# Second half's output projection as seven block products, with sums and scalings made on POOL

## The chip, the cores and the metric

The kernel runs on one core of one Trainium2 chip. TensorE (PE), VectorE (DVE), ScalarE (ACT), GpSimd (POOL) and the DMA issuer SyncE (SP) each work through a queue of their own in order, and wait for one another by semaphores. The metric is the device time of one launch, in microseconds (us), the median of several runs.

## The reference, cut to what matters

One layer with two token mixers over x of 2048 tokens by 2048 features, all in float32:

```python
h = rms_norm(x, norm_w)
q, k, v, z_attn, u, z_ssm = split(h @ w_in)       # 1024, 256, 256, 1024, 1024, 1024 columns
o_attn = swa_sink_attention(q, k, v, ...) * silu(z_attn)
y = gelu(s5_ssm(u, ...));  y = y * sigmoid(y @ w_glu + b_glu)
o_ssm = y * silu(z_ssm)
merged = concat(rms_norm(o_attn, w_a), rms_norm(o_ssm, w_s))   # 1024 + 1024 features
x = x + merged @ w_out                                          # w_out 2048 x 2048
```

Attention looks back over a window of 128 tokens. The state space part runs a linear recurrence over all tokens, done here in 32 pairs of channel groups.

## The kernel before

The tokens are worked in two halves of 1024 (`HT`). Every float32 product is made of three matmuls: each operand is split into a rounded high part and a low rest (`xh`, `xl` for activations, `wh`, `wl` for weights), and high x high, high x low and low x high are added in PSUM. A weight block comes by one DMA on SP's queue into `wr` (ring of three), ACT rounds it into `wh`, DVE subtracts into `wl` (`w_unit`, L308).

A panel is a stretch of such matmuls with one PSUM accumulation: `panel_feat` (L319) has 24 matmuls of 512 columns for each weight block, `panel_tok` (L335) 48 of 256 columns. A panel's four PSUM banks (`psg`) are free again when its results have been read out by its `evac`. Order of the program in `run` (L1021):

- half 0: panels for u, q/k/v and z_attn. Beside them `setup_all` (L1086) prepares the rope tables, the norm of half 1 and the tables of the state space part (`ssm_setup`, L588; its rotation tables start from two small POOL memsets, `Ct` and `St`, L757). Then the z_ssm panels of half 0 and the u panels of half 1, with attention of half 0 beside them (`attend_all`, L499). `x_later` (L295) loads half 1's transposed x in between, scales it by weight and row factor on DVE and splits it.
- half 1: z_attn, q/k/v and z_ssm panels, with `ssm_pairs` (L779) beside them: for each of 32 pairs a load, a split, PE, a scan on DVE, PE again, and a gelu. Its memory pool takes the place of half 0's attention pool.
- the half-GLU of half 0 (`glu`, L911) with `tail_attn` (L880) beside it, the output panels of half 0 (`out_panel`) with attention of half 1 beside them, the half-GLU of half 1 with its `tail_attn`, and at last `out_wide` (L965) for half 1: 4 column blocks x 2 groups of features x 8 weight blocks x 24 matmuls = 1,536 matmuls of 512 columns.

Attention needs POOL: a memset of the first key tile `kst` (L478), the sums `vt` and `dv` (L517 to L520) and the masked product `pm` (L566) are POOL instructions. In the kernel before POOL issues no DMA at all.

"Beside" is set by `weave` (L990): after so many steps of the panels it takes one step of the side work, at a raised priority. A scheduler then fixes, before the program runs, the order of the instructions on each engine's queue; on the chip no engine departs from it.

## Time and profile before

| | us |
|---|---|
| median of three runs (2880.41 to 2883.33) | 2881.29 |
| the profiled execution, its own time | 2882.15 |
| its span on the core | 2880.4 |
| PE busy in the span | 2800.6 |
| DVE, ACT, POOL busy | 1774.8, 1046.9, 154.9 |

The profiled execution lies 0.03% above the median, and 1.75 us of its time lie outside the span. Matmul ends are modelled, so a busy PE is not PE at its peak: the pace is read from the count of matmuls in a stretch. Idle time of an engine that is not the bottleneck costs nothing by itself.

### The profile page before, as it was taken

How to read it: one execution, taken by the hardware profiler on the slowest of the kernel's cores; microseconds unless marked ns; L12 is line 12 of the kernel's file. 1: busy time of each engine (PE TensorE's matmuls, PEld its weight loads, DVE VectorE, ACT ScalarE, POOL GpSimd, SP SyncE). 2: the span in 40 equal slices, each digit the busy share in tenths (PEclk: the TensorE clock that was granted, in tenths of full speed). 3: DMA queues.
4: the chain of work that ended last, by engine and by line, in shares of the span. 5: the costliest groups of instructions: out<-in, count | busy, mean ns of one | idle time of the engine just before them, and what ended most of it. 6: DMA issues, size and time to landing. Idle time of an engine off the chain costs nothing.

```text
span 2880.4 us, 45277 instructions
## 1 busy us (share of the span) xinstructions
PE 2800.6 (97%) x16992; PEld 2502.1 (87%) x16992; DVE 1774.8 (62%) x4171; ACT 1046.9 (36%) x2377; POOL 154.9 (5%) x316
## 2 busy tenths in 40 slices
PE   6999999989999999999999999998999999999999
PEld 5879999878888788888999988878999999778887
DVE  6682746855553955677678984377777755842222
ACT  6411222134552554333333332355555533521110
POOL 0000000001110111000000000000112210000000
PEclk9999999999999999999999999999999999999999
DMA  5842536553332542645355555333444444333321
GB/s 176 241 116 67 158 92 169 144 141 110 98 107 80 184 117 86 164 138 153 119 153 154 160 146 152 107 121 98 148 136 126 125 138 155 99 103 106 106 80 56
DMA packets 421292, 369.36 MB, mean 128 GB/s; under 512 B 53200, under 2 KB 377296, under 8 KB 421072
## 3 DMA queue, kind: packets, MB, share of 16 engines
q1 hardware_dynamic: 419008, 366.45, 43.0%
q8 instruction: 134, 2.20, 0.3%
q14 instruction: 86, 0.70, 0.1%
q10 hardware_dynamic: 2064, 0.01, 0.0%
HBM read 271.03 MB, written 99.55 MB: 129 GB/s over the span
## 4 chain that ended last, share of the span: by engine, by line
PE 77%; DVE 10%; DMA 8%; issue 2%; SPq 2%; ACT 1%; POOL 0%; ACTq 0%; POOLq 0%; DVEq 0%
PE psg L329 30%; PE psg L347 27%; PE psg L974 6%; PE pss L974 3%; DMA oa<-OA 2%; PE pss L531 2%; PE pst L974 2%; PE pso L974 1%; DVE ml L93 1%; DVE yg L84 1%; PE pso L571 1%; PE pso L569 1%; PE pst L557 1%; DVE wl L84 1%; DMA TCS<-St 1%
## 5 line engine op out<-in xcount | busy, mean ns | idle before, releaser
L84 DVE TENSOR_TENSOR wl<-wr,wh 128x512 fp32r<-128x512 f32 x456 | 314.9, 691 | 593.6 <-ACT wh L315 574.5
L315 ACT CAST wh<-wr 128x512 fp32r<-128x512 f32 x456 | 282.1, 619 | 981.4 <-PE psg L329 301.4
L329 PE MATMUL psg<-xh,wl 128*128 128x512 f32 x1536 | 492.9, 394 | 4.8 <-DVE wl L84 4.7
L329 PE MATMUL psg<-xh,wh 128*128 128x512 f32 x1536 | 494.5, 395 | 2.2 <-ACT wh L315 1.3
L329 PE MATMUL psg<-xl,wh 128*128 128x512 f32 x1536 | 493.7, 395 | 2.1 <-DVE xl L84 2.1
L347 PE MATMUL psg<-wl,xh 128*128 128x256 f32 x1536 | 435.1, 284 | 0.9 <-DVE wl L84 0.9
L347 PE MATMUL psg<-wh,xh 128*128 128x256 f32 x1536 | 434.1, 284 | 0.0
L347 PE MATMUL psg<-wh,xl 128*128 128x256 f32 x1536 | 433.5, 284 | 0.0
L329 PEld LDWEIGHTS psg<-xh,wl 128*128 128x128 f32 x1536 | 287.5, 189 | 64.6 <-DVE wl L84 7.4
L329 PEld LDWEIGHTS psg<-xh,wh 128*128 128x128 f32 x1536 | 288.1, 190 | 60.1 <-ACT wh L315 1.8
L329 PEld LDWEIGHTS psg<-xl,wh 128*128 128x128 f32 x1536 | 287.6, 189 | 59.6 <-DVE xl L84 3.6
L347 PE MATMUL psg<-wh,mh 128*128 128x256 f32 x1024 | 289.1, 285 | 7.8 <-ACT tt L922 7.8
L347 PEld LDWEIGHTS psg<-wl,xh 128*128 128x128 f32 x1536 | 294.2, 192 | 1.3 <-DVE wl L84 1.3
L347 PEld LDWEIGHTS psg<-wh,xh 128*128 128x128 f32 x1536 | 293.8, 192 | 0.1
L347 PEld LDWEIGHTS psg<-wh,xl 128*128 128x128 f32 x1536 | 293.5, 192 | 0.0
L347 PE MATMUL psg<-wl,mh 128*128 128x256 f32 x1024 | 290.8, 285 | 0.6 <-DVE wl L84 0.6
L347 PE MATMUL psg<-wh,ml 128*128 128x256 f32 x1024 | 288.8, 285 | 0.0
L347 PEld LDWEIGHTS psg<-wh,mh 128*128 128x128 f32 x1024 | 195.2, 192 | 8.0 <-ACT tt L922 8.0
L347 PEld LDWEIGHTS psg<-wl,mh 128*128 128x128 f32 x1024 | 196.1, 192 | 0.8 <-DVE wl L84 0.8
L347 PEld LDWEIGHTS psg<-wh,ml 128*128 128x128 f32 x1024 | 195.2, 192 | 0.0
L548 ACT ACTIVATE sm<-pss,mx,rs 128x128 f32<-128x128 f32 x240 | 108.4, 458 | 50.3 <-DVE mx L84 49.9
L84 POOL TENSOR_TENSOR pm<-ph,sel 128x256 fp32r<-128x256 f32 x120 | 95.4, 795 | 516.1 <-ACT ph L560 498.6
(403 smaller groups left out, 4662.3 us busy)
## 6 DMA issues: line engine op xcount, KB each, us to landing
wr<-in_w_in_dram SPq DMA_DIRECT2D x296, 256.0 KB
wr<-in_w_out_dram SPq DMA_DIRECT2D x128, 256.0 KB
tb<-TCS SPq DMA_DIRECT2D x64, 256.0 KB
xr<-in_x_dram SPq DMA_DIRECT2D x64, 256.0 KB
out_dram<-xr SPq DMA_DIRECT2D x64, 256.0 KB
raw<-MBC SPq DMA_DIRECT2D x32, 384.0 KB
kst<-KK SPq DMA_DIRECT2D x56, 192.0 KB
xst<-in_x_dram SPq DMA_DIRECT2D x16, 512.0 KB
```

Of the source, the lines that this page charges most:

```text
L84: (eng or self.nc.vector).tensor_tensor(out=out, in0=a, in1=b, op=op)
L93: self.nc.vector.scalar_tensor_tensor(out=out, in0=a, scalar=s, in1=b, op0=op0, op1=op1)
L315: nc.scalar.copy(hi, raw)
L329: nc.tensor.matmul(ps[t], wt[:, kk, :], xx[k][:, t * 512:(t + 1) * 512], start=(k == 0 and i == 0), stop=(k == nkc - 1 and i == 2))
L347: nc.tensor.matmul(o, xx[k][:, sl], wt[:, kk, :], start=(k == 0 and i == 0 and t % 2 == 0), stop=(k == nkc - 1 and i == 2), skip_group_che ...
L531: nc.tensor.matmul(ps[:, h * 256:h * 256 + 256], qst[:, bq % 2, hp * 2 + h, :], kst[:, i, ksl], start=(h == 0 and i == 0), stop=(i == 1), ...
L548: nc.scalar.activation(sm[:, h, :], sc[:, h, :], AF.Exp, scale=rs[:, h:h + 1], bias=negm[:, h:h + 1], accum_out=den[:, h:h + 1])
L557: nc.tensor.transpose(pt[:, h * P:(h + 1) * P], sm[:, h, :], self.ident)
L569: nc.tensor.matmul(po, vst[:, blk, :], pp, start=(i == 0), stop=False)
L571: nc.tensor.matmul(po, dv[:, blk, :], pm[:, i], start=False, stop=(i == 1))
L974: nc.tensor.matmul(ps[t], xx[k0 + k][:, t * P:(t + 1) * P], wt[:, 0, :], start=(k == 0 and j == 0), stop=(k == 7 and j == 2))
```

## The change

The second half's output projection is a 1024 x 2048 by 2048 x 2048 product. Seen as 2 x 2 blocks (token half x feature group on one side, feature group x column half on the other) it had eight block products; now it has seven, each of 512 tokens x 1024 features x 1024 columns, between sums and differences of blocks, as in Strassen's scheme (Winograd's form). Four of the seven need sums of weight blocks (`T1` to `T4`); `out_sums` makes them early, in `setup_all`: 32 units of 256 columns, each with six loads, four stores and four additions, all on POOL and POOL's queue. The rows of the two feature groups have to be scaled before blocks can be mixed, so `attn_scale` multiplies half 1's attention by its row factor and writes it to DRAM (`OAN`), 16 times load, multiply, store, again on POOL; the state space part is scaled on DVE (`form_ssm`). The rest of the operands are formed on DVE and ACT as side work of the products. Half 1's x is scaled by its row factor on POOL as well (`x_scaled`, 16 loads, multiplies, stores to `XN`), and `x_later` only applies the weight. Half 1's attention adds up its squares in `attend` (on POOL) in place of `tail_attn`; that attention is spread over 0.7 of the panels in place of 0.5. In the half-GLU the product with silu(z) is written in natural token order, so that what follows runs on whole rows. In all 384 DMAs are put on POOL's queue: 320 for the weight sums (128 KB each), 32 for x, 32 for attention.

```diff
@@ x_scaled is new, x_later shorter
+    def x_scaled(self, pool, half):
         rb = pool.tile([P, HT], F32, tag="rb", name="rb")
         self.spread(self.rstd[:, half * 8:half * 8 + 8], rb, pool)
         for k in range(NK):
+            x = pool.tile([P, HT], F32, tag="xs", name="xs", bufs=2)
+            self.nc.gpsimd.dma_start(x, self.a["xT"][k * P:(k + 1) * P, half * HT:half * HT + HT])
+            self.tt(x, x, rb, ALU.mult, self.nc.gpsimd)
+            self.nc.gpsimd.dma_start(self.XN[k], x)
+            yield
+
+    def x_later(self):
...
-            self.stt(x, x, self.nw[:, k:k + 1], rb, ALU.mult, ALU.mult)
-            nc.scalar.copy(self.xh[k], x)
-            self.tt(self.xl[k], x, self.xh[k].bitcast(F32), ALU.subtract)
+            self.ld.dma_start(x, self.XN[k])
+            w = self.nw[:, k:k + 1]
+            nc.scalar.activation(self.xh[k], x, AF.Copy, scale=w)
+            self.stt(self.xl[k], x, w, self.xh[k].bitcast(F32), ALU.mult, ALU.subtract)
@@ ssm_setup, in the loop over the rotation tables
+                for _ in range(4):
+                    next(xs, None)
                 yield
@@ new: scaled attention, and its use
+    def attn_scale(self, pool):
+        for k in range(8):
+            for c in (0, 512):
+                o = pool.tile([P, 512], F32, tag="on", name="on")
+                self.nc.gpsimd.dma_start(o, self.OA[k * P:(k + 1) * P, HT + c:HT + c + 512])
+                self.tt(o, o, self.rba[:, c:c + 512], ALU.mult, self.nc.gpsimd)
+                self.nc.gpsimd.dma_start(self.OAN[k, :, c:c + 512], o)
+            yield
+    def form_a11(self):
+        for k in range(8):
+            self.split_to(0, k, self.attn_scaled(k, 0, 512), self.aow[:, k:k + 1])
+            yield
@@ new: weight sums (w_block(q) is a block of w_out for q < 4, else of WT)
+    def out_sums(self, pool):
+        nc = self.nc
+        g = nc.gpsimd
+        for u in range(32):
+            k, c = u // 4, u % 4 * 256
+            x, y = (pool.tile([P, 256], F32, tag=f"ws{i}", name=f"ws{i}") for i in range(2))
+            get = lambda t, q: g.dma_start(t, self.w_block(q, k, c, 256))
+            put = lambda i, t: g.dma_start(self.WT[i, k, :, c:c + 256], t)
+            get(x, 1)
+            get(y, 0)
+            self.tt(x, x, y, ALU.subtract, g)
+            put(0, x)
+            get(y, 3)
+            self.tt(y, y, x, ALU.subtract, g)
+            put(1, y)
+            yield
+            get(x, 2)
+            self.tt(x, y, x, ALU.subtract, g)
+            put(3, x)
+            get(x, 1)
+            get(y, 3)
+            self.tt(y, y, x, ALU.subtract, g)
+            put(2, y)
+            yield
@@ new: one block product
+    def product(self, slot, q, evac, *sides):
...
+            ps = [self.psg() if n == 0 else self.psa() for t in range(4)]
+            for k in range(8):
+                raw = self.wp.tile([P, 512], F32, tag="wr", name="wr")
+                self.ld.dma_start(raw, self.w_block(q, k, n * 512, 512))
...
+                for t in range(4):
+                    sl = slice(o + t * P, o + t * P + P)
+                    for j, (xx, wt) in enumerate(((self.sh[c], hi), (self.sh[c], lo), (self.sl[c], hi))):
+                        nc.tensor.matmul(ps[t], xx[:, sl], wt, start=(k == 0 and j == 0), stop=(k == 7 and j == 2))
...
+            for t in range(4):
+                evac(n, t, ps[t])
@@ new: strassen_out, its seven calls; out_wide is gone
+        self.product(0, B11, e1, (self.form_s3(), 8, 0), (ssm, 5, 6))
+        self.product(1, T3, e7, (ssm, 5, 0), (s2, 3, 10))
+        self.product(2, B21, e2, (s2, 5, 0))
+        self.product(0, T2, e6, (s1, 8, 0))
+        self.product(1, T1, e5, (s4, 8, 0))
+        self.product(2, B22, e3, (a22, 8, 0))
+        self.product(0, T4, e4)
@@ run
-            self.weave(o0[:-1], self.attend_all(pool, 1), 33, 0.0, 0.5, PA)
+            self.asq = pool.tile([P, HT], F32, tag="asq", name="asq")
+            self.weave(o0[:-1], self.attend_all(pool, 1), 33, 0.0, 0.7, PA)
+            self.ra = self.row_scale(pool, self.asq, 1.0, "ra")
...
-            self.weave(o0[-1:])
-            self.glu(1, pool, yin, self.tail_attn(1, pool, 0), 8)
...
+            self.spread(self.ra, self.rba, pool)
...
+            self.weave(o0[-1:], self.attn_scale(pool), 8, 0.0, 1.0, 0)
+            self.glu(1, pool, yin, self.form_a11(), 8)
+            self.strassen_out(pool)
@@ setup_all
-        yield from self.ssm_setup()
+        with self.tc.tile_pool(name="bg", bufs=1) as pool:
+            sums = self.out_sums(pool)
+            for _ in self.ssm_setup():
+                for _ in range(3):
+                    next(sums, None)
+                yield
```

In `strassen_out` a result is read out of PSUM by DVE, added to x on POOL and stored; the last product (`e4`) ends the kernel so.

How the order on the queues changes, at three places. First POOL, from the tables' last memsets to the first attention instructions (`ws` are the tiles of the weight sums, `WT` their place in DRAM). Before:

```order
L757 MEMSET Ct 128x8
L758 MEMSET St 128x8
L478 MEMSET kst 128x2x128
L84 TENSOR_TENSOR vt<-vst 128x128
L84 TENSOR_TENSOR vt<-vt 128x64
L84 TENSOR_TENSOR dv<-vt,dv 128x64
L84 TENSOR_TENSOR vt<-vst 128x192
L84 TENSOR_TENSOR vt<-vt 128x128
```

Now, the last rows ahead of the first attention instruction:

```order
L1007 DMA WT<-ws_6076 128x256
L1006 DMA ws_6075<-in_w_out_dram 128x256
L87 TENSOR_TENSOR ws_6075<-ws_6076,ws_6075 128x256
L1007 DMA WT<-ws_6075 128x256
L1006 DMA ws_6076<-in_w_out_dram 128x256
L1006 DMA ws_6075<-in_w_out_dram 128x256
L87 TENSOR_TENSOR ws_6076<-ws_6076,ws_6075 128x256
L1007 DMA WT<-ws_6076 128x256
L489 MEMSET kst 128x2x128
L87 TENSOR_TENSOR vt<-vst 128x128
L87 TENSOR_TENSOR vt<-vt 128x64
```

All 320 DMAs and 128 additions of the weight sums, and x_scaled, now stand ahead of the memset of `kst`; 15 units and two instructions of the next stand ahead of the first `Ct` memset.

On PE the first attention matmul had 1,066 panel matmuls of 512 columns ahead of it and has 2,444 now; those of 256 columns are 2,304 in both.

Second PE, in `ssm_pairs`, half 1 (`pss` takes the first product of a pair, `pso` or `pst` the second, `psg` a panel; `raw` and `Hh`, `Hl` are a pair's inputs and states). Before, around one pair:

```order
L329 MATMUL psg<-xl_9645,wh 128x512
L805 MATMUL pss<-lo,hi 128x256
L805 MATMUL pss<-hi,lo 128x256
L805 MATMUL pss<-hi 128x256
L805 MATMUL pss<-lo,hi 128x256
L805 MATMUL pss<-hi,lo 128x256
L329 MATMUL psg<-xl_9645,wh 128x512
L329 MATMUL psg<-xh_9644,wl 128x512 x2
L329 MATMUL psg<-xh_9646,wh 128x512
L835 MATMUL pso<-hi 128x256
L835 MATMUL pso<-lo,hi 128x256
L835 MATMUL pso<-hi,lo 128x256
```

Now, around one of the pairs 3 to 13:

```order
L861 MATMUL pso<-Hl,hi 128x256
L861 MATMUL pso<-Hh,lo 128x256
L858 MATMUL pso<-hi 128x256
L858 MATMUL pso<-lo,hi 128x256
L858 MATMUL pso<-hi,lo 128x256
L861 MATMUL pso<-Hh,hi 128x256
L861 MATMUL pso<-Hl,hi 128x256
L861 MATMUL pso<-Hh,lo 128x256
L828 MATMUL pss<-hi 128x256
L828 MATMUL pss<-lo,hi 128x256
L828 MATMUL pss<-hi,lo 128x256
L828 MATMUL pss<-hi 128x256
```

Attention of half 0 stands later, and the pairs, whose memory it holds, begin later in the panels. From the first matmul of pair 3 to the first matmul of the first q panel PE's queue now holds 241 matmuls of pairs and of key transposes, and no panel matmul; before, panel matmuls stood between any two pairs.

Third DVE, at the same place (`A`, `B`, `S`, `H`, `gt`, `y`, `lo` are steps of a pair, `wl` a weight block's low part, `zt` a z panel). Before, from one pair to the next:

```order
L84 TENSOR_TENSOR wl<-wr,wh 128x512
L93 SCALAR_TENSOR_TENSOR y<-gt,pso 128x512
L817 SCALAR_TENSOR_TENSOR S<-r_628,A 128x256 x2
L84 TENSOR_TENSOR A_13307<-S,tb 128x512
L84 TENSOR_TENSOR B_13308<-S,tb 64x512 x2
L84 TENSOR_TENSOR wl<-wr,wh 128x512
L93 SCALAR_TENSOR_TENSOR H<-B_13308,sgn,A_13307 128x2x255
L84 TENSOR_TENSOR Hl<-H,Hh 128x512
L84 TENSOR_TENSOR wl<-wr,wh 128x512
L84 TENSOR_TENSOR A<-pss,tb 128x512
L84 TENSOR_TENSOR B<-pss,tb 64x512 x2
L84 TENSOR_TENSOR lo<-raw,hi 128x2x256
```

Now:

```order
L96 SCALAR_TENSOR_TENSOR gt<-gt,pst 128x512
L96 SCALAR_TENSOR_TENSOR A<-B,sgn,A 128x512
L840 SCALAR_TENSOR_TENSOR S<-r_631,A 128x256
L96 SCALAR_TENSOR_TENSOR y<-gt,pst 128x512
L840 SCALAR_TENSOR_TENSOR S<-r_631,A 128x256
L87 TENSOR_TENSOR A_13026<-S,tb 128x512
L87 TENSOR_TENSOR B_13027<-S,tb 64x512 x2
L96 SCALAR_TENSOR_TENSOR H<-B_13027,sgn,A_13026 128x2x255
L87 TENSOR_TENSOR Hl<-H,Hh 128x512
L87 TENSOR_TENSOR A<-pss,tb 128x512
L87 TENSOR_TENSOR B<-pss,tb 64x512 x2
L87 TENSOR_TENSOR lo<-raw,hi 128x2x256
```

The weight steps between the pairs are gone: eleven pairs stand in a row, followed by the second half of the k panel's steps and the four `vs` subtractions that free the v panel's PSUM banks, for which the first q panel waits.

## Rows read from the trace of the kernel before

**Rows 1.** the page: engine totals, DVE and the granted clock by slices.

```profile
PE 2800.6 (97%) x16992; PEld 2502.1 (87%) x16992; DVE 1774.8 (62%) x4171; ACT 1046.9 (36%) x2377; POOL 154.9 (5%) x316
DVE  6682746855553955677678984377777755842222
PEclk9999999999999999999999999999999999999999
```

**Rows 2.** the page: the chain that ended last, its shares by engine.

```profile
PE 77%; DVE 10%; DMA 8%; issue 2%; SPq 2%; ACT 1%; POOL 0%; ACTq 0%; POOLq 0%; DVEq 0%
```

**Rows 3.** stretches: their us, then PE, PEld, DVE, ACT, POOL busy, granted clock, DMA.

```profile
2600.00:2800.00 200.00, 200.00 (x884) 165.65 (x883) 50.91 (x77) 23.08 (x37) 0.00 (x0) 1.00 0.34 102
2470.00:2530.00 60.00, 49.71 (x211) 39.14 (x210) 51.52 (x60) 35.91 (x47) 0.00 (x0) 0.94 0.22 68
1900.00:2000.00 100.00, 86.84 (x514) 76.96 (x513) 80.46 (x121) 50.80 (x71) 3.03 (x6) 0.97 0.36 107
```

**Rows 4.** POOL's groups by form: busy us, mean ns; idle before, releasers.

```profile
L84 POOL TENSOR_TENSOR pm<-ph,sel 128x256 fp32r<-128x256 f32 x120 | 95.4, 795 | 516.1 <-ACT ph L560 498.6 <-DVE pss L538 8.6 <-DVE mx L84 8.2
L84 POOL TENSOR_TENSOR vt<-vst 128x192 f32<-128x192 f32 x28 | 17.3, 617 | 438.8 <-DMA q<-QS 227.7 <-DMA vst<-VS 211.0
```

**Rows 5.** DMAs in the chain that ended last: start, us, transfer.

```profile
456.46 4.01 DMA RK<-L
938.14 3.82 DMA ZS<-zt
2159.55 4.24 DMA vst<-VS
```

**Rows 6.** DVE in time: the last update of the output.

```profile
2875.39 0.75 DVE L93 SCALAR_TENSOR_TENSOR xr<-pst,rsr,xr 128x512 f32<-128x512 f32 x1
```

**Rows 7.** the page: ACT rounds a weight block (busy, mean ns, idle before).

```profile
L315 ACT CAST wh<-wr 128x512 fp32r<-128x512 f32 x456 | 282.1, 619 | 981.4 <-PE psg L329 301.4
```

**Rows 8.** POOL's instructions in time: start, length, line; idle before and its releaser.

```profile
123.48 0.22 POOL L638 MEMSET PR<- 128x64 f32 x1 [47.08 <-DMA wr<-in_w_in_dram]
460.74 0.11 POOL L757 MEMSET Ct<- 128x8 f32 x1 [290.58 <-DMA wr<-in_w_in_dram]
596.99 0.31 POOL L478 MEMSET kst<- 128x256 f32 x1 [36.42 <-DMA TCS<-St]
601.39 0.45 POOL L84 TENSOR_TENSOR vt<-vst 128x128 f32<-128x128 f32 x1 [4.09 <-DMA vst<-VS]
```

**Rows 9.** SP's DMA issues in time, around the start of attention.

```profile
598.03 0.59 SPq L482 DMA_DIRECT2D vst<-VS  x1
```

**Rows 10.** PE in time: the first score matmuls, and two 256-column panel matmuls.

```profile
610.37 0.59 PE L531 MATMUL pss<-kst,qst 128*128 128x256 f32 x3
...
2395.03 0.28 PE L347 MATMUL psg<-wh,mh 128*128 128x256 f32 x1
2395.15 0.28 PE L347 MATMUL psg<-wl,mh 128*128 128x256 f32 x1
```

**Rows 11.** the stretch 1300 to 1400 us, columns as in rows 3.

```profile
1300.00:1400.00 100.00, 100.00 (x618) 90.08 (x617) 74.33 (x115) 32.55 (x58) 0.61 (x6) 1.00 0.50 145
```

**Rows 12.** DVE groups by form in that stretch: busy us, mean ns; idle before.

```profile
L84 DVE TENSOR_TENSOR wl<-wr,wh 128x512 fp32r<-128x512 f32 x16 | 11.0, 690 | 13.4 <-ACT wh L315 13.1
L84 DVE TENSOR_TENSOR Hl<-H,Hh 128x512 fp32r<-128x512 f32 x6 | 4.2, 692 | 3.7 <-ACT Hh L829 3.7
L93 DVE SCALAR_TENSOR_TENSOR zt<-zt,psg 128x512 f32<-128x512 f32 x6 | 3.9, 682 | 0.0
```

**Rows 13.** tile acca: form, count, ns min/median/max, starts.

```profile
L84 DVE TENSOR_TENSOR acca<-acca,oa x14: 1206/1225/1227, 1874.1 to 2499.9; 128x1024 f32<-128x1024 f32 x14
```

**Rows 14.** DVE in time: a small step of a norm.

```profile
2539.38 0.17 DVE L90 TENSOR_SCALAR rsm<-pst 128x8 f32<-128x8 f32 x1 [0.90 <-PE pst L855]
```

More of the change, by code (lines that the diff above doesn't have):

```diff
@@ L583, in attend @@
                 t0 = (b - 1) * P
+                if half:
+                    sq = pool.tile([P, 2, 256], F32, tag="sq", name="sq")
+                    nc.scalar.activation(sq, oT, AF.Square)
+                    acc = self.asq[:, t0 - HT:t0 - HT + 256]
+                    if g == 0:
+                        self.tt(acc, sq[:, 0], sq[:, 1], ALU.add, nc.gpsimd)
+                    else:
+                        for c in range(2):
+                            self.tt(acc, acc, sq[:, c], ALU.add, nc.gpsimd)
                 self.st.dma_start(self.OA[g * 256:g * 256 + 256, t0:t0 + 256].rearrange("(c p) t -> p c t", p=P), oT)
@@ new lines, in strassen_out, with part, rows, final @@
+    def strassen_out(self, pool):
+        nc = self.nc
+        acc = {}
+        def part(n, c, t):
+            i = (8 * c + 4 * n + t) // 2
+            if i not in acc:
+                acc[i] = self.xt.tile([P, HT], F32, tag=f"x{'hl'[i // 4]}{12 + i % 4}", name=f"ac{i}")
+            return acc[i][:, (t % 2) * 512:(t % 2) * 512 + 512]
+        e = lambda n, t: part(n, 0, t)
+        v = lambda n, t: part(n, 1, t)
+        def rows(y, r, c, n, t):
+            r0 = HT + r * 512 + t * P
+            return y[0, r0:r0 + 2 * P, c * 1024 + n * 512:c * 1024 + n * 512 + 512].rearrange("(t p) c -> p t c", p=P)
+        xs = {}
+        def final(r, c, n, t, ps, base, keep, op=ALU.add):
+            if t % 2 == 0:
+                x = self.stage("xr").rearrange("p (t c) -> p t c", t=2)
+                xs[0] = x, (self.stage("xo").rearrange("p (t c) -> p t c", t=2) if keep else x)
+            x, o = xs[0]
+            v = o[:, t % 2] if keep else base
+            self.tt(v, base, ps, op)
+            if t % 2 == 0:
+                self.ld.dma_start(x, rows(self.a["x"], r, c, n, t))
+            self.tt(x[:, t % 2], x[:, t % 2], v, ALU.add, nc.gpsimd)
+            if t % 2:
+                self.st.dma_start(rows(self.out, r, c, n, t - 1), x)
+        def e1(n, t, ps):
+            nc.scalar.copy(e(n, t), ps)
+        def e7(n, t, ps):
+            self.tt(v(n, t), e(n, t), ps, ALU.add)
+        def e2(n, t, ps):
+            final(0, 0, n, t, ps, e(n, t), True)
+        def e6(n, t, ps):
+            self.tt(e(n, t), e(n, t), ps, ALU.add)
+            self.tt(v(n, t), v(n, t), ps, ALU.add)
+        def e5(n, t, ps):
+            self.tt(e(n, t), e(n, t), ps, ALU.add)
+            final(1, 1, n, t, ps, v(n, t), True)
+        def e3(n, t, ps):
+            final(0, 1, n, t, ps, e(n, t), False)
+        def e4(n, t, ps):
+            final(1, 0, n, t, ps, v(n, t), False, ALU.subtract)
+        def ssm_side():
+            self.rss = self.row_scale(pool, self.gacc, 0.125, "rs")
+            yield
+            self.rbs = pool.tile([P, HT], F32, tag="rba", name="rbs")
+            self.spread(self.rss, self.rbs, pool)
+            yield
+            yield from self.form_ssm()
+        B11, B12, B21, B22, T1, T2, T3, T4 = range(8)
+        ssm, s2, s1 = ssm_side(), self.form_s2(), self.form_s1()
+        s4, a22 = self.form_view(2, 0), self.form_view(0, 1)
+        self.product(0, B11, e1, (self.form_s3(), 8, 0), (ssm, 5, 6))
[5 more added lines that the diff above has]
+        self.product(0, T4, e4)
@@ L939, in glu @@
             pass
+        if half:
+            self.yg, self.gacc = out, acc
+            return
         for m in range(8):
-            self.split(k0 + m, yg[m], self.sow[:, m:m + 1], True)
+            self.split(k0 + m, out[m], self.sow[:, m:m + 1])
         self.rss = self.row_scale(pool, acc, 0.125, "rs")
@@ L1078, in run, with x_next @@
                 self.ld.dma_start(ap, getattr(self, n))
[L1080 removed]
+    def x_next(self):
         self.x_alloc()
[L1082 removed]
+        self.x_later()
         return
```

147 lines of the change are left out of this document (96 added, 51 removed).

## The prediction

> **What bounds the kernel now.** I read the page's totals first: PE is busy for 97% of the span, and its clock is granted at nine tenths or more in every slice; the slices of DVE show where there is room beside it, and the last tenth is nearly free of DVE work [rows 1]. The chain that ended last lies on PE for 77%, with 10% on DVE and 8% on DMAs [rows 2]. Then I read stretches, for the pace of PE and for the places where it is short. In the last product PE executes 884 matmuls of 512 columns in 200 us, 0.2262 us each: this stretch is PE at its limit, so fewer matmuls there are time saved. At 2470 to 2530 it executes 211 where 60 / 0.2262 = 265 would fit, so 54 x 0.2262 = 12.2 us are lost; at 1900 to 2000, in the half-GLU of half 0, it is idle for 13.2 us, with DVE busy for 80 [rows 3]. So the change removes work from the engine that bounds, and the question is what it puts in the way of that engine. The sum starts from the profiled execution, 2882.2 us, which is 0.03% above the median; no term depends on that.
>
> **The change part by part. The product.** 1,536 matmuls become 7 blocks of 192, 1,344; a block is 192 x 0.2262 = 43.4 us. One block less: **-43.4**.
>
> Forming the operands and the weights is now done in 2.71 us for each weight block (12 matmuls) in place of 5.4. The ring of three gives a block 8.1 us. The longest load among the chain's DMAs took 4.24 us [rows 5], ACT's cast takes 0.62 [rows 7] and DVE's subtraction 0.69 [rows 12]: 5.6, so it is hidden as long as SP and DVE come to it at once. They also serve scaled attention and its splits. If the load took twice the 4.24, a block would need 9.8 / 3 = 3.26 us, 112 x 0.55 = 61 us more. I take **+10**, with ends 0 and +61, since DVE had only 51 of 200 us of work there [rows 3].
>
> The end: the last four banks go to DVE and then one after another to POOL. POOL's 128x256 product takes 0.795 us [rows 4], so I estimate 1.6 for 512 columns; 4 x 1.6 less the 4 x 0.75 of DVE that they replace [rows 6], and a store of twice the size: **+4**.
>
> The half-GLU: half 0's strided steps on DVE become whole rows; of the 13.2 us idle in a hundred I give back **-8** (0 to -13). In that of half 1 the 12.2 lost us could return, as tail_attn is gone, but its place is taken by POOL's chain for OAN. Each of 16 pieces is a load, a product, a store, and the next load waits for that store: 2 x 3.8 + 1.6 + 0.6 = 9.8 us (3.8 is explained below). The chain begins in the last output panel of half 0, some 31 us before its end by the order, and the first half of its last row is there 15 x 9.8 - 31 = 116 us after, where PE, with 384 + 84 matmuls ahead, would want it at 106. So 10 of the 12.2 are lost again: **-2**. Half 1's x saves DVE sixteen products beside panels: 0, hidden by PE; if DVE were late there, it would be a gain.
>
> Subtotal: 2882.2 - 43.4 + 10 + 4 - 8 - 2 = **2842.8**.
>
> **POOL's queue ahead of attention.** This is the first large debt. One unit of the weight sums has six round trips that nothing overlaps: the pair of loads, the load of y, that of x, the store that frees x, a pair of loads, and the store that frees y for the next unit. The kernel before shows no DMA on POOL. The nearest row is SP's 128 KB load of vst: issued at 598.03 [rows 9], POOL's sum starts on it at 601.39 [rows 8], 3.36 us; the other end is the 4.24 of the 192 KB load [rows 5]; RK (4.01) and ZS (3.82) lie between. I take the middle, 3.8, since the loads here also share the DMA engines with the weight stream. A unit is 6 x 3.8 + 4 x 0.795 for its additions [rows 4] + 2 x 0.59 for issues that no round trip covers [rows 9] = 27.2 us, and 32 of them 869. The 16 products of x (4 x 0.795 = 3.2 each, 51 in all) stand in the order between a unit's load and its addition, partly inside round trips; I take half, 26, with ends 0 and 51. POOL starts after the PR memset's wait, at 123.5 [rows 8], since only two loads stand ahead of that. So kst is written at 123.5 + 869 + 26 = 1018.6.
>
> When does PE want it? The first score matmul ran at 610.4 [rows 10], 13 us behind kst's memset [rows 8]. By the order 2,444 - 1,066 = 1,378 more panel matmuls now stand ahead of it: 610.4 + 1378 x 0.2262 = 922. POOL is late by **+97**, and PE's queue is in order, so panels behind it wait too. At 3.36 a round trip it is +12, at 4.24 it is +181; a round trip of 3.3 us breaks even. The lateness shows first at the tables: 15 units stand ahead of the first Ct memset, 123.5 + 15 x 27.2 = 531 against 460.74 [rows 8], and DVE, which builds the tables in order between weight steps, would wait there, and PE behind it. Both are the same delay, counted once.
>
> A page's price stands apart from the sum. The Trainium skill ("DMA: Bandwidth & Descriptors", section "Anatomy of one DMA — SWDGE (gpsimd) path") puts a DMA issued by POOL at about 2.0 us plus its bytes at 436 GB/s, an estimate of 2.3 us for 128 KB. By it a unit would take 18.2 us, POOL would be done at 732, and the 97 would be nothing; no run here shows a DMA of POOL, and SP's row of the same size shows 3.36 us.
>
> **The burst of pairs.** This is the second. By the order PE has 241 matmuls of pairs and transposes in a row, with no panel matmul between, and DVE eleven pairs in a row. In the stretch 1300 to 1400, with six pairs beside panels, DVE was busy for 74.3 us [rows 11], of which 11.0 were weight steps and 3.9 z's [rows 12]: (74.3 - 11.0 - 3.9) / 6 = 9.9 us of DVE for a pair, and 3.7 / 6 = 0.6 waiting for ACT's Hh [rows 12]. So 11 x 10.5 = 115.5. Then the k panel's remaining steps and the vs subtractions, for which the first q panel's banks wait: 6 of 0.69, 3 of 1.22 (estimated from a sum of 128x1024 [rows 13]) and 14 small ones of 0.17 [rows 14], 10 us. Together 125.5, during which PE does only 241 x 0.12 = 29 us of its own (0.12 is the step of two 256-column matmuls [rows 10]; these are that size or smaller, so it isn't more than that unless they wait). Before, those 29 lay between panels and count in PE's total, so the debt is **+96**. From below, a few steps of the first pairs can run while attention still holds PE: 85; from above, a pair whose transfers through DRAM (3.8 to 4.2 us each) are not covered by the next pair: 130.
>
> **Sum:** 2842.8 + 97 + 96 = 3035.8; forecast **3036**.
>
> **The rivals.** *POOL in time* (0.23): the round trip is 3.3 us or less and POOL is done before 922. For: vst's 3.36 is close, and includes SP's issue. Against: three of four rows are longer. The burst stays: 2842.8 + 96 = **2939**. This is also the way the skill's price would have it; it has the same chance.
>
> *POOL much later* (0.10): the round trip is 4.6 us or more, because POOL's own generation of a transfer is dearer than SP's or because it queues behind the weight stream. A unit is 32 us, POOL is done at 1173: +251, **3190**; at 5 us 3267.
>
> *The other side, faster* (0.06): the burst costs little. DVE's pairs would have to run at 5.4 us or less (11 x 5.4 + 10 - 29 = 40, the point where the gain of the product is used up) and POOL be in time. That needs pairs ahead of their place in DVE's queue, in the time in which attention leaves DVE idle, and the memory that they share with attention speaks against it. Fully hidden: **2843**. The same, or the seven blocks not being paced by PE, could end near 2882 (0.01).
>
> **How the numbers follow.** The forecast, a late POOL and the burst, has 0.60. Its own range goes from 2843 + 85 + 12 = 2940 to 2843 + 130 + 181 = 3154. The range reaches down to POOL in time with the burst, 2930, and up to 3165 with part of the +61 of the weight loads; that leaves out the much later POOL, the faster case and the same, 0.17. A measurement of this kernel can tell about 0.2% (6 us) from no change: faster 0.06, same 0.01, slower 0.93.
>
> **What the profile after would show.** Seven blocks of 43.4 us in the last 310 us, PE at over 95%: else the +10 was too small. POOL's timeline: the time from a ws load's issue to the addition on it is the round trip; 3.8 is right, 2.3 the page's. kst's memset near 1019, and ahead of it a first score matmul that waits for POOL (or DVE for Ct, near 530). A stretch of about 125 us behind attention in which PE is busy for some 30 and DVE nearly all of it, with a wait of the first q panel for DVE. A PE wait for OAN of about 10 us at the start of the products. Wrong would be: PE gaps mostly elsewhere, a granted clock that falls behind the gaps, so that panels run slower than 0.2262 us (then the time is above my sum), or pairs that PE finishes in the shadow of attention.

## The result: 3106.7 us, and the profile after

The changed kernel takes 3106.73 us (3104.82 to 3110.59) beside 2882.31 for the kernel before in the same comparison: 1.078 times as long, 95% interval 1.077 to 1.080. The forecast was 3036 with a range of 2930 to 3165.

From the page of the kernel after: totals, the slices of DVE and POOL and of the granted clock, and the shares of the chain that ended last (compare [rows 1, 2]).

```profile
PE 2807.7 (90%) x16832; PEld 2504.9 (81%) x16832; DVE 1871.3 (60%) x4271; ACT 1082.9 (35%) x2453; POOL 631.0 (20%) x920
DVE  6673652961113255555688899735778775556753
POOL 0133333653333211111100000000022231220112
PEclk9999996999998699999955999999999999999999
PE 51%; DMA 26%; DVE 8%; POOL 7%; issue 5%; ACT 1%; SPq 1%; POOLq 0%; ACTq 0%; DVEq 0%
```

PE is as busy as before (2807.7 us), in a span that is 226 us longer. The chain no longer lies on PE for 77% but for 51%, and DMAs and POOL have a third of it; by the page's lines 11% are transfers of `ws` and 4% of `WT`, which did not exist. The granted clock, at nine tenths or more in every slice before, falls where PE has stood: at about 470 to 540, 930 to 1090 and 1550 to 1710 us (a slice is 77.7 us).

The stages are bounded by first and last starts of matmuls. First the kernel before (form, count, ns min/median/max, first to last start in us; the last column is its forms):

```profile
L329 PE MATMUL psg<-yh,wh x256: 387/389/504, 1860.7 to 2510.5; 128*128 128x512 f32 x128
L347 PE MATMUL psg<-wh,mh x1024: 274/283/580, 1955.2 to 2417.7; 128*128 128x256 f32 x171
```

and after, score matmuls, half-GLU and output panels of half 0:

```profile
L542 PE MATMUL pss<-kst,qst x512: 274/281/562, 1063.6 to 2583.0; 128*128 128x256 f32 x171
L340 PE MATMUL psg<-yh,wh x256: 389/389/396, 2111.6 to 2760.2; 128*128 128x512 f32 x128
L358 PE MATMUL psg<-wh,mh x1024: 274/283/583, 2198.7 to 2673.9; 128*128 128x256 f32 x171
```

| stretch | before | after | more | forecast |
|---|---|---|---|---|
| start to the first score matmul, with 1,378 x 0.2262 = 311.7 us of panels moved ahead of it | 610.4 [rows 10] | 1063.6 | +141.5 | +97 |
| from there to the half-GLU of half 0, without these 311.7 | 1250.3 | 1048.0 | +109.4 | +96 |
| half-GLU of half 0 | 94.5 | 87.1 | -7.4 | -8 |
| output panels of half 0 | 462.5 | 475.2 | +12.7 | 0 |
| half-GLU of half 1, products, end | 462.7 | 432.2 | -30.5 | -31.4 |

In the second row the 311.7 us are taken off the stage before, as these panels now run ahead of it. The sum is 225.7 us, the difference of the spans. So two terms ahead of the half-GLU make all of the loss, and they are the two that were forecast.

**POOL's queue.** POOL in time: the first load of the sums, the first `Ct` memset and the end of the sums (start, length, line; in brackets the idle time ahead and what ended it), which answers to [rows 8]:

```profile
129.43 1.29 POOL L1006 DMA_DIRECT2D ws<-in_w_out_dram  x2 [52.60 <-DMA lim<-in_a_imT_dram]
...
513.67 0.54 POOL L1006 DMA_DIRECT2D ws<-in_w_out_dram  x1 [1.42 <-DMA WT<-ws]
514.20 0.13 POOL L778 MEMSET Ct<- 128x8 f32 x1
...
1003.78 0.54 POOL L1006 DMA_DIRECT2D ws<-in_w_out_dram  x1 [1.41 <-DMA WT<-ws]
...
1008.34 0.54 POOL L1006 DMA_DIRECT2D ws<-in_w_out_dram  x1
1011.33 0.72 POOL L87 TENSOR_TENSOR ws<-ws,ws 128x256 f32<-128x256 f32 x1 [2.45 <-DMA ws<-in_w_out_dram]
...
1017.26 0.57 POOL L1007 DMA_DIRECT2D WT<-ws  x1 [0.41 <-POOL ws L87]
1019.81 0.54 POOL L1006 DMA_DIRECT2D ws<-in_w_out_dram  x1 [1.45 <-DMA WT<-ws]
...
1026.30 0.54 POOL L1006 DMA_DIRECT2D ws<-in_w_out_dram  x1 [1.51 <-DMA WT<-ws]
...
1048.25 0.31 POOL L489 MEMSET kst<- 128x256 f32 x1 [1.67 <-DMA WT<-ws]
```

The waits for the load and for the store are to be seen one by one. A load issued at 1008.34 is added at 1011.33, 2.99 us later; a store issued at 1017.26 lets the next load of its tile go at 1019.81, 2.55 us later. A unit here takes 1026.30 - 1003.78 = 22.5 us. From issue to landing, the page's DMA part gives these medians (count, KB each, us):

```profile
ws<-in_w_out_dram POOLq DMA_DIRECT2D x192, 128.0 KB, 3.0
WT<-ws POOLq DMA_DIRECT2D x128, 128.0 KB, 2.2
```

kst is written at 1048.25 (forecast 1018.6) and the first `Ct` at 514.20 (forecast 531). Who waited, first PE, then DVE, then SP's queue (us in total, times, longest):

```profile
PE pst L501 <- DMA zT<-ZA: 71.3, 1, 71.3
PE psg L358 <- DVE wl L87: 44.9, 2, 43.1
DVE Ct L87 <- POOL St L779: 42.3, 1, 42.3
SPq L492 <- DMA ws<-in_w_out_dram: 68.2, 3, 65.2
```

The tables came first: DVE stood 42.3 us for the `St` beside `Ct`, and PE 43.1 of 44.9 us for the weight step behind that on DVE. Then PE stood 71.3 us at the first transposes of attention. Their loads stand behind kst's on SP, and kst's (L492) wait 65.2 us in one piece for a load of `ws`, whose memory attention's tiles take over. These two waits of PE are 114 of the 141 us.

**The row of pairs.** The stretch of ten pairs, columns as in [rows 3]:

```profile
1569.50:1688.90 119.40, 55.70 (x179) 41.88 (x180) 102.83 (x159) 32.29 (x58) 1.02 (x10) 0.50 0.43 125
```

119.4 us for ten pairs, 11.94 each, with 179 matmuls; DVE is busy for 102.8, and the granted clock is at 0.50, the lower of its two levels (1.2 GHz). PE stands for more than half of it. The last panel matmul ahead of the row and the first behind it are 156.3 us apart:

```profile
1558.62 0.28 PE L358 MATMUL psg<-wh,xl 128*128 128x256 f32 x1
1714.92 0.28 PE L358 MATMUL psg<-wh,xh 128*128 128x256 f32 x1
```

One pair on DVE, then on ACT and PE (start, length, line, idle ahead):

```profile
1587.60 0.75 DVE L96 SCALAR_TENSOR_TENSOR H<-B,sgn,A 128x510 f32<-128x510 f32 x1
1589.09 0.69 DVE L87 TENSOR_TENSOR Hl<-H,Hh 128x512 fp32r<-128x512 f32 x1 [0.74 <-ACT Hh L852]
1592.39 1.83 DVE L87 TENSOR_TENSOR lo<-raw,hi 128x512 fp32r<-128x512 f32 x3 [0.60 <-ACT hi L817]
```

```profile
1591.73 0.62 ACT L817 CAST hi<-raw 128x512 fp32r<-128x512 f32 x1 [2.68 <-PE pso L861]
1589.11 0.58 PE L861 MATMUL pso<-Hh,hi 128*128 128x256 f32 x1 [3.14 <-ACT Hh L852]
1590.22 0.41 PE L861 MATMUL pso<-Hh,lo 128*128 128x256 f32 x1
1590.43 0.41 PE L858 MATMUL pso<-hi 128*128 128x256 f32 x1
```

The first block is DVE's; the second has a line of ACT and four of PE. DVE waits twice in a pair, 0.74 us for ACT's `Hh` and 0.60 for ACT's `hi`. PE steps 0.21 us from one matmul to the next, where [rows 10] has 0.12.

**The products.** Seven blocks and the end took 432 - 87 = 345 us with the half-GLU's 87 taken off, 7 x 43.4 = 304 of it at PE's pace. The forecast wait for OAN is there (SP's wait, then PE's):

```profile
SPq L945 <- DMA OAN<-on: 19.4, 3, 11.8
2783.92 2.07 PE L1050 MATMUL psg<-wh,fh 128*128 128x512 f32 x4 [7.96 <-ACT wh L1044]
```

### The profile page after: what moved, and what is told of

The parts are those of the page before. It is cut to its first block, busy times and chain, and to the rows that moved or that the text cites. A ratio compares the mean times of both kernels' runs of the same rounds, so it can differ in the third digit from the quotient of the medians.

```text
span 3106.1 us, 46045 instructions
## 1 busy us (share of the span) xinstructions
PE 2807.7 (90%) x16832; PEld 2504.9 (81%) x16832; DVE 1871.3 (60%) x4271; ACT 1082.9 (35%) x2453; POOL 631.0 (20%) x920
## 4 chain that ended last, share of the span: by engine, by line
PE 51%; DMA 26%; DVE 8%; POOL 7%; issue 5%; ACT 1%; SPq 1%; POOLq 0%; ACTq 0%; DVEq 0%
PE psg L340 18%; PE psg L358 18%; DMA ws<-in_w_out_dram 11%; DMA WT<-ws 4%; PE psg L1050 4%; POOL ws L87 3%; PE pss L1050 2%; PE pss L542 2%; DMA on<-OA 2%; DMA OAN<-on 2%; DMA xs<-in_xT_dram 2%; POOL xs L87 1%; DMA XN<-xs 1%; POOL WT L1007 1%; PE pso L1050 1%
## 5 line engine op out<-in xcount | busy, mean ns | idle before, releaser
L87 DVE TENSOR_TENSOR wl<-wr,wh 128x512 fp32r<-128x512 f32 x504 | 363.4, 724 | 632.8 <-ACT wh L326 517.0
L326 ACT CAST wh<-wr 128x512 fp32r<-128x512 f32 x392 | 242.3, 619 | 787.9 <-PE psg L340 428.3
L358 PE MATMUL psg<-wl,xh 128*128 128x256 f32 x1536 | 436.8, 285 | 43.1 <-DVE wl L87 43.1
L87 POOL TENSOR_TENSOR ws<-ws,ws 128x256 f32<-128x256 f32 x128 | 120.8, 944 | 322.4 <-DMA ws<-in_w_out_dram 322.3
```

The source lines that it names most:

```text
L87: (eng or self.nc.vector).tensor_tensor(out=out, in0=a, in1=b, op=op)
L326: nc.scalar.copy(hi, raw)
L358: nc.tensor.matmul(o, xx[k][:, sl], wt[:, kk, :], start=(k == 0 and i == 0 and t % 2 == 0), stop=(k == nkc - 1 and i == 2), skip_group_che ...
```

## The experiments

All ratios are to the kernel before, measured beside the kernel in question. The three kernels `no_sums...` read plain blocks of w_out in place of the sums, so they don't compute the layer; they are here for their times alone.

| kernel | us | ratio (95%) |
|---|---|---|
| x_undone | 3075.1 | 1.067 (1.065 to 1.069) |
| no_sums | 2879.2 | 0.999 (0.998 to 1.000) |
| no_sums_x_undone | 2851.7 | 0.990 (0.989 to 0.991) |
| no_sums_x_plain | 2860.9 | 0.993 (0.991 to 0.995) |
| sums_y2 | 3052.9 | 1.061 (1.059 to 1.062) |
| sums_at_pairs | 3025.9 | 1.049 (1.047 to 1.051) |
| sums_at_pairs_x_undone | 3028.1 | 1.051 (1.050 to 1.053) |
| sums_at_pairs_h | 3014.0 | 1.046 (1.044 to 1.048) |
| sums_4t | 2902.1 | 1.008 (1.006 to 1.009) |
| sums_4t_x_undone | 2891.0 | 1.004 (1.003 to 1.005) |
| sums_4t_x_undone_oan | 2889.7 | 1.003 (1.002 to 1.005) |
| sums_4t_pairs_h_x_undone | 2859.1 | 0.993 (0.992 to 0.994) |

**What the parts cost by themselves.** `no_sums`:

```diff
-            sums = self.out_sums(pool)
             for _ in self.ssm_setup():
-                for _ in range(3):
-                    next(sums, None)
                 yield
@@ w_block
-            return self.WT[q - 4, k, :, c0:c0 + n]
+            q -= 4
```

> The weight sums are left out, and the four products that need them read plain blocks of w_out in their place, so the output is not the layer's; all else stays (x scaled on POOL, seven products, scaled attention on POOL). Theory: all of the loss ahead of the half-GLU comes from POOL's sums, lateness and burst both; attention is at its old place in the order (1,127 panel matmuls ahead). From the stages of the changed kernel behind 2111 us (half-GLU -7, half 0's output +13, second half-GLU -7, products -24): 2882 - 25 = 2857, range 2845 to 2870. Rival: the scalings of x on POOL, or the new order of the first half, cost by themselves: above 2900.

Measured 2879.2: without sums the whole loss is gone, lateness and row of pairs both, but 22 us more than expected remain. That is outside both ranges; part of the theory holds, and part of the rival. The first score matmul ran at 662.4 with 61 more panel matmuls ahead than before, 38 us late. x scaled on POOL was the suspect, and `no_sums_x_undone` takes it back to DVE:

```diff
@@ x_later
-            self.ld.dma_start(x, self.XN[k])
-            w = self.nw[:, k:k + 1]
-            nc.scalar.activation(self.xh[k], x, AF.Copy, scale=w)
-            self.stt(self.xl[k], x, w, self.xh[k].bitcast(F32), ALU.mult, ALU.subtract)
+            self.ld.dma_start(x, self.a["xT"][k * P:(k + 1) * P, half * HT:half * HT + HT])
+            self.stt(x, x, self.nw[:, k:k + 1], rb, ALU.mult, ALU.mult)
+            nc.scalar.copy(self.xh[k], x)
+            self.tt(self.xl[k], x, self.xh[k].bitcast(F32), ALU.subtract)
```

> No weight sums (the four products read plain blocks in their place, so the output is not the layer's) and x scaled on DVE as in the kernel before: what is left is the seven products, the scaled attention on POOL and the new half-GLU. Theory: without sums the x chain held attention back (first score matmul at 662 with 1,127 panels ahead, 38 us late, and the half-GLU began 28 us after that of the kernel before); with it gone the half-GLU begins near 1861, and the total is 2879 - 28 = 2851. Rival: those 28 us are the order's own, not x's: 2870 to 2880.

Measured 2851.7. So the seven products with everything but sums and x are worth 28.5 us, and x on POOL costs some 27 even with no sums beside it (27.5 between the two medians; 25.4 by what each kernel gains on the kernel before beside it). `no_sums_x_plain` keeps x's transfers on POOL's queue and drops only the product:

```diff
@@ x_scaled
-            self.tt(x, x, rb, ALU.mult, self.nc.gpsimd)
```

> As no_sums (no weight sums, plain blocks in their place), and the 16 products of x by its row factor on POOL are left out too; its 32 transfers on POOL's queue stay, so x comes unscaled by that factor and the output is not the layer's. Theory: x cost 28 us because POOL's products, 2.4 us alone, were drawn out to up to 11 us beside DVE's rotation tables (operations on two SBUF tiles back to back), and drew those out in turn; without the products attention starts within 12 us of the panels' pace and the total is within 8 us of no_sums_x_undone: 2850 to 2860. Rival: it is the 512 KB transfers, serial on POOL's queue: 2868 or more.

Measured 2860.9: by the medians 18 of the 27.5 us go with the products, and 9 with the rest of the move (its 32 transfers, and the other way of scaling x in `x_later`). The kernel before differs by up to 2.7 us between these measurements, so the shares are good to some 3 us. The time lies between the theories, and each held a part. How a product on POOL gets so dear is to be seen in the changed kernel: POOL, two products of x, and DVE at the same time (start, length, line).

```profile
645.90 14.22 POOL L87 TENSOR_TENSOR xs<-xs,rb 128x1024 f32<-128x1024 f32 x2 [3.42 <-DMA xs<-in_xT_dram]
```

```profile
651.56 1.22 DVE L87 TENSOR_TENSOR tv<-Ct,us 128x1024 f32<-128x1024 f32 x1
...
654.43 1.28 DVE L96 SCALAR_TENSOR_TENSOR zt<-zt,psg 128x512 f32<-128x512 f32 x2
655.62 2.23 DVE L87 TENSOR_TENSOR Ct<-Ct,tu 128x1024 f32<-128x1024 f32 x1
657.78 3.42 DVE L87 TENSOR_TENSOR St<-St,tv 128x1024 f32<-128x1024 f32 x1
```

Two products that take 2.4 us each alone took 14.22. Up to 654 DVE runs operations on two SBUF tiles without a gap; then come two that read PSUM (`zt`), and right behind them DVE's own table steps take 2.23 and 3.42 us in place of 1.22. In `x_undone`, at the same place, an addition of the sums shows it too:

```profile
518.97 0.76 POOL L87 TENSOR_TENSOR ws<-ws,ws 128x256 f32<-128x256 f32 x1 [2.24 <-DMA ws<-in_w_out_dram]
525.96 10.64 POOL L87 TENSOR_TENSOR ws<-ws,ws 128x256 f32<-128x256 f32 x1 [2.77 <-DMA ws<-in_w_out_dram]
```

```profile
535.31 0.69 DVE L87 TENSOR_TENSOR wl<-wr,wh 128x512 fp32r<-128x512 f32 x1
```

0.76 us one time, 10.64 the next. The last line is the end of DVE's operations on two SBUF tiles, which ran without a gap all through the second addition: it ended at 536.00, and POOL's addition at 536.60. The Trainium skill ("SBUF — State Buffer", section "Who interferes with whom") says that a DVE instruction with two inputs in SBUF contends with a POOL instruction that reads SBUF, since its second input comes through a read interface that the two share, and calls the shared ports an exclusive lock. These rows agree in both directions; that it is this port and nothing else was not tested apart.

**Whether POOL's time is made of round trips.** `sums_y2` gives one of the two tiles a second buffer, so one of a unit's six serial trips is gone:

```diff
-            x, y = (pool.tile([P, 256], F32, tag=f"ws{i}", name=f"ws{i}") for i in range(2))
+            x, y = (pool.tile([P, 256], F32, tag=f"ws{i}", name=f"ws{i}", bufs=1 + i) for i in range(2))
```

> The changed kernel with a second buffer for one of the two tiles of the sums (y), so that a unit's first loads no longer wait for the last store of the unit before: five serial round trips in place of six. Theory: a unit is 2.6 us shorter (22.4 to 19.8 where POOL is undisturbed), 32 of them 80 us; the order wants the first score matmul after 2,266 panel matmuls, 40 us earlier than in the changed kernel (2,444), and has a row of 196 matmuls of pairs in place of 241 (two pairs, 24 us): the lateness falls from 141 to about 100 and the row's debt from 109 to about 90: 3107 - 60 = 3047, range 3030 to 3070. Rival: POOL's time is not made of round trips: same as the changed kernel.

Measured 3052.9. kst came 79 us earlier (969.17), the first score matmul ran at 983.9 with 2,266 panel matmuls ahead: 983.9 - 610.4 - 1200 x 0.2262 = 102 us late; from there to the half-GLU 90 us are lost, with two pairs fewer in the row (no panel matmul from 1530.0 to 1655.8, 125.8 us in place of 156.3). One trip of 2.5 us, 32 times, moved the kernel by 54 us, at both terms as worked out. This is the run that carries the explanation: round trips make POOL late, and where the order asks for attention earlier, the row of pairs without panels is shorter.

**x in the changed kernel.** `x_undone` (the edit of x above, sums as they were):

> x_scaled undone: half 1's x is scaled on DVE as in the kernel before; the weight sums stay where they are. Theory 1: the 16 scalings of x cost POOL about 107 us (in the changed kernel units 16 to 18 of the sums took 179 us where 72 would do), so kst's memset comes near 940 in place of 1048; PE's order has 2,152 panel matmuls of 512 columns ahead of the first score matmul, so PE wants it at 610.4 + 1086 x 0.2262 = 856, late by some 100; no row of pairs without panels is left in the order, but a row of 383 matmuls of attention: 2940 to 3000. Rival (the forecast's own price of x, 26 us): kst near 1020, and under 3% is gained, 3060 to 3080. The wait of DVE for Ct near 514 stays about 40 us under both.

kst in POOL's time:

```profile
971.49 0.30 POOL L490 MEMSET kst<- 128x256 f32 x1 [1.62 <-DMA WT<-ws]
```

971.5 in place of 1048.3, and POOL began 2 us earlier, so x cost POOL some 75 us, between the two theories. But the kernel gained only 32, as the rival had it. The order had moved too: it now wanted attention after 2,152 panel matmuls, so PE was 986.2 - 610.4 - 1086 x 0.2262 = 130 us late in place of 141; and 89 us were lost behind it, now beside a row of 383 matmuls of attention without panels in place of a row of pairs. An engine that is faster by 75 us is of use only as far as the fixed order does not ask for it earlier.

**Sums where POOL is free.** `sums_at_pairs` moves the sums to the pairs of half 1 (they leave the setup, and the pairs' `raw` has one buffer in place of two):

```diff
+    def pairs_and_sums(self):
+        with self.tc.tile_pool(name="sw", bufs=1) as pool:
+            sums = self.out_sums(pool)
+            for _ in self.ssm_pairs():
+                for _ in range(2):
+                    next(sums, None)
+                yield
+            for _ in sums:
+                pass
```

> The weight sums are moved from the setup to the side of ssm_pairs, one unit for each pair, where POOL has only a small memset for each pair; to make room raw has one buffer in place of two there. Theory: POOL's queue ahead of attention is the cause, not the sums as such: 2857 as without sums, plus what the pairs lose: a pair's memset of H stands behind up to one or two round trips of 2.6 to 3.0 us, with 25 us for a pair beside panels: 2857 to 2890. Rival: the sums' traffic (42 MB) or POOL's additions beside DVE slow the pairs or the panels: above 2900.

> The sums beside the pairs as in sums_at_pairs, and in addition x scaled on DVE as in the kernel before. Theory: where POOL is not late, its scalings of x cost next to nothing, so this is within 6 us of sums_at_pairs. Rival: x on POOL beside the rotation tables holds DVE and PE by itself: faster than sums_at_pairs by 15 us or more.

Measured 3025.9 and 3028.1: far off. Attention stood where it stands without sums, but the half-GLU began at 2020 where it began at 1889 without sums. The two lie 2 us apart, as expected of them, but with the half-GLU held like this that says nothing of what x costs. I took the pairs' `H` memset on POOL for the cause, and `sums_at_pairs_h` moves it:

```diff
-                nc.gpsimd.memset(H[:, :, 0:1], 0.0)
+                nc.vector.memset(H[:, :, 0:1], 0.0)
```

> As sums_at_pairs, with one instruction moved: the memset of a pair's first state column (H) is on DVE in place of POOL, so POOL has nothing for the pairs while it makes the sums. Theory: sums_at_pairs lost 132 us in the pairs' stretch (the half-GLU began at 2020 where it began at 1889 without sums) because each pair's memset of H stood in POOL's queue behind a unit of 22 us, and each unit behind the pair's store: with the memset gone from POOL, 2880 to 2900, as no_sums plus 0 to 20. Rival: the sums' transfers or POOL's additions slow DVE's pairs: above 2950.

Measured 3014.0: the theory fell as an account of the time, but the memset had held the pairs. From `sums_at_pairs`, waits of ACT and PE between 1150 and 2020 us:

```profile
ACT Hh L862 <- POOL H L858: 272.9, 30, 21.3
PE pst L871 <- ACT Hh L862: 57.4, 11, 14.7
PE pso L871 <- ACT Hh L862: 26.9, 11, 7.1
```

ACT waited 272.9 us for POOL's memset, in 30 pieces, and PE 84 us for what ACT makes next. In `sums_at_pairs_h` these 84 us of PE's are 1.9, so the pairs are free, and the waits of PE and SP in the same stretch name what takes their place:

```profile
PE psg L340 <- ACT wh L326: 136.3, 1, 136.3
SPq L1149 <- DMA ws<-in_w_out_dram: 138.2, 3, 135.3
```

One wait of 136 us and no other to speak of. The sums last until 2007 (32 x 27 us beside the pairs, from 1153), and the half-GLU's pool takes their memory, so its loads on SP wait for the last `ws`, as the loads of attention did in the changed kernel. In `sums_at_pairs` the sums lasted until 1998, so there the half-GLU could not begin much earlier either, with slowed pairs or without. The time is where the rival had it, above 2950, but not for its reason: here PE hardly waits for the pairs. It is again 32 times the unit.

**A shorter unit.** `sums_4t` loads four blocks at once into four tiles, and then adds and stores four times. To make room for the tiles, `tq` of the setup shares the memory of `tm` (those lines are not shown):

```diff
-            get(x, 1)
-            get(y, 0)
-            self.tt(x, x, y, ALU.subtract, g)
-            put(0, x)
...
+            for i, q in enumerate((1, 0, 3, 2)):
+                g.dma_start(b[i], self.w_block(q, k, c, 256))
+            made(b[1], b[0], b[1], 0)
+            made(b[0], b[2], b[0], 2)
+            yield
+            made(b[2], b[2], b[1], 1)
+            made(b[3], b[2], b[3], 3)
```

> The sums stay in the setup on POOL and on POOL's queue, but a unit has four tiles: four loads go out together, then four additions, each with its store (256 DMAs in place of 320, and no load waits behind a store within a unit). Theory: the time of a unit is its six serial round trips (22 to 24 us); with one load wait and about one store wait it is 4 x 0.55 + 2.4 + 4 x 1.7 + 1.5, about 13 us; 25 units stand ahead of the first Ct memset and are done near 450, so no wait of 40 us for Ct, the first score matmul within 50 us of the panels' pace, and no row of pairs: 2880 to 2900, as no_sums. Rival: POOL's additions beside DVE, or its DMA queue's rate, set the unit: 18 us or more, Ct late by over 50 us, above 2930.

> As sums_4t, and x scaled on DVE as in the kernel before. Theory: the seven products then bring their gain: 2851 (as without sums and with x undone) plus 0 to 12 for POOL's last sums beside the rotation tables: 2851 to 2863, faster than the kernel before by about 1%. Rival: sums beside the tables cost as x did: 2875 or more.

> As sums_4t_x_undone, and attn_scale makes the first token halves of all eight rows before the second halves, since the first operand (form_a11) needs only those. Theory: the first product's wait for OAN (in the changed kernel SP waited 19 us for it, PE about 10 for the weight block queued behind on SP) goes: 8 to 10 us less than sums_4t_x_undone. Rival: the second halves are then late for the next operand (form_s3), and under 3 us are gained.

Measured 2902.1, 2891.0 and 2889.7. The unit fell to some 11 us where it is undisturbed (in the second kernel units begin their additions at 205.09, 216.00 and 226.67 us), and 205 of the 224 us were won back by the first alone; the row of pairs is gone. But all are slower than forecast, the first by 2 us, the second by 28 at least: its first score matmul ran at 650.3 with 24 more panel matmuls ahead than before, 34 us late. The stretch 150 to 250 us without sums and x on POOL (columns as in [rows 3]):

```profile
150.00:250.00 100.00, 94.34 (x501) 81.40 (x500) 60.88 (x240) 15.94 (x30) 0.85 (x1) 0.97 0.32 93
```

and in `sums_4t_x_undone`:

```profile
150.00:250.00 100.00, 85.77 (x399) 71.79 (x400) 74.06 (x237) 16.93 (x31) 65.99 (x98) 0.91 0.62 187
```

For nearly as many instructions (237 and 240) DVE is busy for 74 us in place of 61, and PE issues 399 matmuls in place of 501. This is the setup of the state space part, which POOL's additions now run into. The shared memory of `tq` is a rival for this loss, but the last kernel below shares it too, with no additions there, and is at the old pace:

```profile
150.00:250.00 100.00, 94.24 (x499) 81.26 (x498) 60.40 (x238) 15.84 (x30) 0.85 (x1) 0.95 0.31 92
```

The edit of the order of OAN gained nothing that can be told, as its rival had it: between 2520 and 2640 us PE's wait of 9.4 us for the first weight block is gone, but 14 us of waits for weights come a little later, where there were 6.

`sums_4t_pairs_h_x_undone` puts the parts together: four tiles, beside the pairs, `H` on DVE, x on DVE.

> All three together: four tiles for a unit of sums (11 us in place of 22), sums beside the pairs, H's memset on DVE, and x scaled on DVE as in the kernel before. Theory: nothing of POOL's is on anyone's way ahead of the products: 2852 (as without sums and with x undone) plus 0 to 10 for DMAs and the single raw buffer: 2852 to 2862, about 1% faster than the kernel before. Rival: the single raw buffer or the traffic beside the pairs costs 15 us or more: above 2867.

Measured 2859.1, 0.993 of the kernel before (0.992 to 0.994): 0.7% faster than the kernel before, and 248 us faster than the changed one. Its loads of the sums, its first score matmul and the start of its half-GLU (count, ns, first to last start):

```profile
L1015 POOL DMA_DIRECT2D ws<-in_w_out_dram x128: 536/544/746, 1170.5 to 1552.5; - x128
L543 PE MATMUL pss<-kst,qst x512: 274/281/386, 611.0 to 2334.3; 128*128 128x256 f32 x171
L341 PE MATMUL psg<-yh,wh x256: 389/389/396, 1868.2 to 2510.4; 128*128 128x512 f32 x128
```

The sums run from 1170 to 1558, attention is where it was (611.0), and the half-GLU begins 7.5 us later than in the kernel before. No run has these sums beside the pairs with the memset of `H` left on POOL, so what that part is worth here is open.

## Why the forecast was right, point by point

- **Direction, range and the two debts** held. The sum ahead of the half-GLU was forecast at +193 and came at +251; all behind it was forecast at -39 and came at -25.
- **Lateness of POOL, +97 forecast, +141 measured: the path was right, and the size came near in part by luck.** The term of the round trip was too large: 3.8 us, where a load took 2.99 and a store 2.55, so an undisturbed unit takes 22.5 and not 27.2. With the other terms as they stood, 129.4 + 32 x 22.5 + 26 = 875, POOL would have been in time for 922, which was my rival: the round trip did come below its 3.3. What I left out made up for it: from 129.4 to 1048.3 are 919 us, 720 of them undisturbed units. x took some 75 (x_undone) in place of 26, and the 124 that remain lie beside the setup, the tables and the panels; in x_undone, with no x on POOL, it is 844 for the same 720. Additions drawn out are a part of them (128 take 120.8 us, where 128 x 0.72 is 92), the rest longer transfers and waits for tables; I have not taken them apart. So the units were 149 us too dear, and 173 were missing elsewhere. I had bounded x by its time alone (51), with no row for POOL beside DVE on the same tiles; [rows 4] came from a stretch where they rarely meet.
- The same sum set kst's memset against the time of the score matmul, though it names the 13 us between the two: by its own numbers it should have said +110. And POOL's queue was not the only thing that held attention. SP's loads waited for the sums' memory until the same last stores, which was in no term.
- "The lateness shows first at the tables", "counted once": right in kind. The 43 us at Ct did not come on top of POOL's end, which alone sets the first score matmul (15 us behind kst, 13 before).
- **The row of pairs, +96 forecast, +109 measured for the whole stretch to the half-GLU.** The row itself cost more: 156.3 us without a panel matmul where the sum had 125.5, so 127 with the 29 of PE's own taken off. Elsewhere in the stretch 18 were won back (no_sums, without a row, wins 10 there), which was in no term, so that 96 and 109 lie close together is in part luck. Of the 31 us that the row was short, 16 are the eleven pairs, 11.94 us each in place of 10.5: DVE 10.3 (9.9 forecast), `Hh` 0.74 (0.6), 0.60 for ACT's rounding of the next pair's inputs, which I did not have, and 0.3 in short gaps. ACT's step waits for PE's last matmul of the pair, and PE goes at 0.21 a step there. The other 15 lie at the ends of the row, above all behind the last pair.
- **The clock.** That it would be low in the row was not in the sum; a clock that falls behind the gaps was named as a sign of being wrong. It fell, but panels paid little: behind the wait of 71 us matmuls of 512 columns came every 0.43 us from 1056.4 to 1058.9, and every 0.23 us from 1059.4 on. The pairs paid.
- **A block less, -43.4, with +10, +4, -2:** -30.5 measured beside -31.4, the wait for OAN included (8 us in one piece, 10 forecast). So beside the block 13 us were lost where the three terms make 12; no run takes them apart. no_sums_x_undone gave 2851.7 where the subtotal said 2842.8.
- **Half-GLU of half 0:** -7.4 for -8. **Output panels of half 0:** +12.7 where I had nothing; no_sums_x_undone has +9 there as well, so it does not come from the sums. The change's attention of half 1 is the likely place (its squares on POOL, or its later spread); no run separates them.
- **x moved off DVE, "0, hidden by PE":** wrong, and the price was on POOL and on whatever DVE does beside it: some 27 us without the sums.
- **The price that the forecast quotes** from the Trainium skill ("DMA: Bandwidth & Descriptors", section "Anatomy of one DMA — SWDGE (gpsimd) path"), an estimate of 2.3 us for a 128 KB transfer on POOL's queue: the stores' 2.2 us from issue to landing bear it out, the loads take 3.0. The result that hung on it, POOL in time, did not come, for what stood beside the transfers and not for their price.

## What to carry to other kernels

A chain load, add, store on one in-order queue costs its round trips and not its bytes: count the waits that nothing overlaps, and let a unit load all it needs before the first result; here that took a unit from 22.5 to some 11 us. Work that is off everyone's path is still on the path of whatever comes behind it on that queue and of whatever takes its memory: ask for both, and for the time by which they are wanted. When a move takes away one wait, look for the next in line: freeing the pairs of the memset only uncovered the wait for the sums' memory. When a fixed order holds side work back, its price comes twice, once as the wait and once where the held work then stands with nothing beside it.

## What the runs showed of the hardware that was not expected

- A POOL addition of 128x256 took 0.72 us alone (changed kernel) and up to 10.64 beside DVE operations on two SBUF tiles without a gap (x_undone); a DVE operation of 1.22 us took 3.42 beside POOL (changed kernel).
- In the changed kernel a load of 128 KB on POOL's queue took 3.0 us from issue to landing, a store 2.2 (medians); issuing one held POOL for 0.54 to 0.57 us.
- In the row of pairs, with PE standing for more than half of the time, the granted clock was 0.50 for 119 us; matmuls of 256 columns came every 0.21 us.
